# mLSTM gate scans behind the first query and key projection, a gate tile in front of the last head, the last head's end behind the first z tiles

## The chip, the core and the metric

The kernel runs on one core of a Trainium2 chip. The core's engines each work through a queue of their own, in order: TensorE (PE; its weight loads are shown apart, as PEld), VectorE (DVE), ScalarE (ACT), GpSimd (POOL) and SyncE (SP), which only issues transfers. Semaphores tie the queues together. The metric is the time of one execution on the device, in microseconds (us).

## The reference

One layer of a diffusion backbone: 1024 latent tokens and 256 context tokens of width 1024, in float32. The tokens are modulated, projected once into all branch inputs, mixed by a bidirectional mLSTM (8 heads) and a bidirectional gated linear attention (GLA, 4 heads), merged through gates, and passed through a gated convolutional feed-forward network, with two layer norms. The part that matters here is the mLSTM, cut from the reference:

```
q_m, k_m = split(silu(short_conv(concat([q_m, k_m]), conv_qk)))     # 3 taps along the tokens
i_f, i_b, f_f, f_b = transpose(g_m.reshape(b, t, 4, 8))             # 4 gate rows per head
mlstm_gates = ((i_f, log_sigmoid(f_f)), (i_b, log_sigmoid(f_b)))

def step(carry, inp):                        # one chunk of tokens of one head
    b = cumsum(lfc)
    dlog = where(tril, b[:, None] - b[None, :] + lic[None, :], -inf)
    m_inter = b + m
    m_row = maximum(m_inter, dlog.max(-1))
    s = (qc @ kc.T) * exp(dlog - m_row[:, None])
    w_inter = exp(m_inter - m_row)
    num = w_inter[:, None] * (qc @ c_mat) + s @ vc
    den = w_inter * (qc @ n_vec) + s.sum(-1)
    h = num / maximum(abs(den), exp(-m_row))[:, None]
    ...                                      # new c_mat, n_vec, m
y_m = (head_norm(h_m, mlstm_norm_g) * sigmoid(o_m)) @ w_branch_mlstm
y_g = (head_norm(h_g, gla_norm_g) * silu(z_g)) @ w_branch_gla
out = (sigmoid(gate_a) * y_m + sigmoid(gate_b) * y_g) @ w_out
```

## The kernel before

All products of float32 data are made of three: each operand is split into a high part (rounded to the format that TensorE takes) and a low part, and high x high, high x low and low x high are added in one bank of PSUM (`mm3`, lines 279 to 285). The high part of a weight is written by ScalarE (line 252), the low part by VectorE (line 253). `wload` fetches a block of weights as four quarters, through four raw buffers (`raw`) and six buffers each of high and low parts (`whi`, `wlo`). A projection of 128 columns over 512 tokens is 24 products; the context's 256 tokens make 24 of half the width.

PSUM has four kinds of banks with two each: `pj` and `pa` mainly for projections, `pt` for transposes, `po` for the outputs of the heads. A bank is free again when VectorE or ScalarE has read it.

The order of the work is that of the Python code as a list scheduler lays it out: it fills each engine's queue by priority and by when it believes an operand will be ready, so instructions of neighbouring steps are interleaved. On the chip each queue is then fixed, and an instruction that waits holds up all behind it on its engine.

Around the change the code does this:

- Four GLA heads, with gate tiles as filler. A gate tile (`gate_tile`, called by `fill`) projects 128 columns of one of the merge gates over all latent tokens: 48 products, two evacuations on ScalarE (line 537) and two stores. There are 16, four of them here. The last half head of the GLA, `finish`, is kept in the list `rest` and run by `late()`.
- `ml_proj_v(0)`, the values of the first two mLSTM heads (240 products).
- `ml_gates()`: the gate rows of all heads and both directions, on 64 partitions. VectorE makes the running maximum and sum by scans (lines 456 to 462), then `ra` (464), `rr` (466), the key factors `wk` (472, 473; Exp on ScalarE, 474) and the row factors `re` (477, 478). `rr`, `re` and the decays are written to DRAM (489 to 491). TensorE turns three of the row tables by 30 small transposes (501) into `ta`, `twk` and `tem`, which VectorE copies from six `pt` banks (502).
- `ml_proj_qk(h)`, queries and keys of a head: two projections for q, three for k. ScalarE evacuates each (732), VectorE adds two taps of the convolution out of the same bank (727), ScalarE takes the tanh (747) and VectorE multiplies it on (748).
- `ml_scan(h)`: masks and `rr` rows are fetched by GpSimd's queue and added (760, 761), the `re` rows broadcast (764); Exp on ScalarE (765, 769), GpSimd multiplies q (766); TensorE transposes k (777), makes the scores (786), the states (796) and the outputs (816, 817); VectorE normalizes (837). Its last part, `finish`, is given back: eight transposes (844), two scaled copies on ScalarE (845), a store (847).
- The loop over the eight heads projects head h+1, runs the end of head h-1 (`late()`), scans head h, and fills with one or two gate tiles. Then `gated` projects the z tiles (two per block of weights), multiplies the GLA heads with them and splits the products; a stage with the GLA branch weights follows, in which modulation weights are summed on VectorE (906, 908), and later `gated` again for the o gates of the mLSTM heads.

Names in the rows: `s` is any of the numbered slots, `u` the buffers of the tokens, `qq` and `kk` two double slots (row tables first, then the scaled queries and keys of a head), `s<-rmask`, `s<-rr` and `qq<-re` the transfers of a head's masks, rows and row factors.

Of the kernel before, what the change touches and what calls it, by code (L numbers as in the profile page):

```python
# [24 lines left out]
MH = 8  # L25
# [11 lines left out]
def layer_kernel(ctx, tc, I, out, dbg=None):  # L37
# [16 lines left out]
    def nm(s):  # L54
        cnt[0] += 1
        return f"{s}_{cnt[0]}"

    def pt(tag, shape):
        return ps.tile(shape, F32, tag=tag, name=nm(tag))
# [4 lines left out]
    def slot(i, shape, dt=F32):  # L64

        if i in (8, 9, 10, 11) and sl is sl0:
            n = 1
            for w in shape[1:]:
                n *= w
            tag = "kk" if i < 10 else "qq"  # L70
            if i % 2 == 0:
                half[tag] = sl.tile([P, 2, n], dt, tag=tag, name=nm(tag))
            v = half[tag][0:shape[0], i % 2, :]
            return v if len(shape) == 2 else v.rearrange("p (a b) -> p a b", b=shape[2])
        return sl.tile(shape, dt, tag=f"s{i}", name=nm(f"s{i}"))

    def ubt(i, shape, dt=F32):
        return ub.tile(shape, dt, tag=f"u{i}", name=nm(f"u{i}"))
# [35 lines left out]
    for l in range(7):  # L114
        h = 1 << l
# [91 lines left out]
    for i in range(2):  # L207
        hi = stg.tile([P, 2, 256], F32R, tag="whi", name=nm("whi"), bufs=6)
        lo = stg.tile([P, 2, 256], F32R, tag="wlo", name=nm("wlo"), bufs=6)
        h, l = (t[:].rearrange("p a (b c) -> p (a b) c", c=P) for t in (hi, lo))  # L210
# [17 lines left out]
    def cB(i):  # L228
        return colB[:, i:i + 1]
# [21 lines left out]
    def split(hi, lo, src, eng=G):  # L251
        A.activation(hi, src, AF.Copy)  # L252
        eng.tensor_tensor(lo, src, hi.bitcast(F32), op=ALU.subtract)  # L253

    def wload(segs, nk=KD, k0=0, eng=V, into=None):
        parts = []
        for k4 in range(0, nk, 2):
            n = min(2, nk - k4)
            raw = stg.tile([P, 2, 256], F32, tag="raw", name=nm("raw"), bufs=4)
            r0 = (k0 + k4) * P  # L260
            wid = 0
            for src, c0, w, dst in segs:
                SY.dma_start(raw[:, 0:n, dst:dst + w],
                             src[r0:r0 + n * P, c0:c0 + w].rearrange("(k p) c -> p k c", p=P))
                wid = max(wid, dst + w)
            if into is None:
                hi = stg.tile([P, 2, 256], F32R, tag="whi", name=nm("whi"), bufs=6)
                lo = stg.tile([P, 2, 256], F32R, tag="wlo", name=nm("wlo"), bufs=6)
            else:
                hi, lo = (t[k4 // 4][:, k4 % 4:k4 % 4 + 2, :] for t in into)  # L270
            split(hi[:, 0:n, 0:wid], lo[:, 0:n, 0:wid], raw[:, 0:n, 0:wid], eng)
            parts.append((hi, lo))

        def w(k, c, n):
            hi, lo = parts[k // 2]
            return hi[:, k % 2, c:c + n], lo[:, k % 2, c:c + n]
        return w

    def mm3(p, lhs, rhs, nk=KD):
        for k in range(nk):  # L280
            lh, ll = lhs(k)
            rh, rl = rhs(k)
            T.matmul(p, lh, rh, start=k == 0, stop=False)  # L283
            T.matmul(p, lh, rl, start=False, stop=False)  # L284
            T.matmul(p, ll, rh, start=False, stop=k == nk - 1)  # L285
# [29 lines left out]
    def u_tok(t):  # L315
        if t < 8:
            return lambda k: (uh[k][:, t * P:(t + 1) * P], ul[k][:, t * P:(t + 1) * P])
        o = (t - 8) * P
        return lambda k: (cuh[k // 4][:, k % 4, o:o + P], cul[k // 4][:, k % 4, o:o + P])
# [3 lines left out]
    def proj(w, c, b, tag="pj"):  # L323
        p = pt(tag, [P, 512])
        mm3(p[:, 0:BW[b]], lambda k: w(k, c, P), u_blk(b))
        return p
# [183 lines left out]
    def vbias(off):  # L510
        t = sc.tile([P, 256], F32, tag="vb", name=nm("vb"), bufs=2)
        SY.dma_start(t[:], b_in[off:off + 256].unsqueeze(0).to_broadcast([P, 256]))
        return t
# [18 lines left out]
    def gate_tile(dst, off, cb0, j, tags=("pj", "pj")):  # L532
        w = wtile(w_in, off + j * P)
        for b in range(2):
            p = proj(w, 0, b, tags[b])
            t = sc.tile([P, 512], F32, tag="gt", name=nm("gt"), bufs=2)
            A.activation(t[:], p[:], AF.Identity, scale=0.5, bias=cB(cb0 + j))
            A.dma_start(dst[j][:, b * 512:b * 512 + 512], t[:])
# [163 lines left out]
    def ml_proj_v(pr):  # L702
        w = wload([(w_in, O_VM + pr * 256, 256, 0)], eng=V)
        vb = vbias(O_VM + pr * 256)
        vs = [slot(2 + i, [P, 10, 129]) for i in range(2)]
        for t in vs:
            G.memset(t[:, :, 128:129], 1.0)
        for t0 in range(0, 10, 2):
            p = pt("pj", [P, 2, 256])
            for i in range(2):  # L710
                mm3(p[:, i, :], u_tok(t0 + i), lambda k: w(k, 0, 256))
            for e in range(2):
                V.tensor_tensor(vs[e][:, t0:t0 + 2, 0:P], p[:, :, e * P:(e + 1) * P],
                                vb[:, e * P:(e + 1) * P].unsqueeze(1).to_broadcast([P, 2, P]), op=ALU.add)
        return vs
# [136 lines left out]
    def late():  # L852
        while rest:
            rest.pop()()
# [3 lines left out]
    def fill(n, tags=("pj", "pj")):  # L858
        for _ in range(n):
            gate_tile(*gates.pop(0), tags)  # L860
# [10 lines left out]
        if h:  # L871
            fill(1)
    v2 = ml_proj_v(0)
    rr_d, re_d, decb, (ta, twk, tem) = ml_gates()
    qk = ml_proj_qk(0)
    late()
    for h in range(MH):
        nxt = ml_proj_qk(h + 1) if h + 1 < MH else None
        if h and h % 2 == 0:
            v2 = ml_proj_v(h // 2)  # L880
        late()
        rest.append(ml_scan(h, *qk, v2[h % 2]))
        qk = nxt
        fill(2 if h < 2 or h > 5 else 1, ("pj", "pa"))
    late()
    while gates:
        fill(1)

# [6 lines left out]
    def ytag():  # L895
        seq[0] += 1
        return tags[seq[0] % 3]
# [19 lines left out]
    def gated(off, cb0, src_d, silu):  # L917
        hi, lo = [], []
        for j2 in range(4):
            w = wload([(w_in, off + j2 * 256, 256, 0)])  # L920
            for e in range(2):
                j = 2 * j2 + e
                hi.append(slot(j, [P, SEQ], F32R))
                lo.append(slot(8 + j, [P, SEQ], F32R))
                hr = ubt(16 + j % 2, [P, SEQ])
                SY.dma_start(hr[:], src_d[j][:])
                ht = ubt(18, [P, SEQ])
                zz2 = ubt(19, [P, 2, 512]) if silu else None
                for b in range(2):
                    s_ = slice(b * 512, b * 512 + 512)  # L930
                    p = proj(w, e * P, b, ytag())
                    th = sc.tile([P, 512], F32, tag="gt", name=nm("gt"), bufs=2)
                    A.activation(th[:], p[:], AF.Tanh, scale=0.5, bias=cB(cb0 + j))
                    hs = hr[:, s_]
                    if silu:
                        zt = zz2[:, b, :]
                        A.activation(zt, p[:], AF.Identity, scale=0.5, bias=cB(cb0 + j))
                        V.tensor_tensor(hs, zt, hs, op=ALU.mult)
                    V.scalar_tensor_tensor(ht[:, s_], th[:], 1.0, hs, op0=ALU.add, op1=ALU.mult)
                    split(hi[j][:, s_], lo[j][:, s_], ht[:, s_])  # L940
        return hi, lo

    ya_d = [drt(f"ya{j}", [P, SEQ]) for j in range(8)]
    ghi_, glo_ = gated(O_ZG, c_zg, hg_d, True)
    accs = {}
    for j2 in range(4):
# [33 lines left out]
    bup = colF[0][:, 0:44]  # L980
    cb = colF[0][:, 44:66]
    mhi_, mlo_ = gated(O_OM, c_om, hm_d, False)
    xhi, xlo = [], []
    for j2 in range(4):
# [265 lines left out]
    for j, c in enumerate(todo[len(main):]):  # L1250
        if j >= 6:
            if j < 10:
                h = (ubt(10 + j - 6, [P, 2, 512], F32R) if j < 8 else
                     fin.tile([P, 2, 512], F32R, tag="gl", name=nm("wlate"), bufs=2))
                h = [h[:, 0, :], h[:, 1, :]]
            else:
                h = [fin.tile([P, 512], F32R, tag="z1", name=nm("wlate"), bufs=4)[:] for _ in range(2)]
# [40 lines left out]
```

## Time and profile before

| | |
|---|---|
| three runs | 2292.91 us median (2291.26 to 2295.82) |
| the profiled execution | 2294.39 us, of which the span from first to last instruction is 2292.6 |
| TensorE | busy 2235.5 us, 98% of the span; mean granted clock 0.992 |
| VectorE, ScalarE, GpSimd | busy 58%, 32%, 11% |
| transfers | 246.55 MB, 108 GB/s over the span |

A row of the timeline has the start, the time from the first start to the last end, the engine, line and operation, what is written and read, and in brackets how long the engine stood idle before it and whose end released it. TensorE's products overlap: a row of one product shows 0.39 us, but the next one starts 0.23 later. The granted clock is a share of 2.4 GHz; 0.5 is 1.2 GHz.

### The profile page before, as it was taken

How to read it: one execution, taken by the hardware profiler on the slowest of the kernel's cores; microseconds unless marked ns; L12 is line 12 of the kernel's file. 1: busy time of each engine (PE TensorE's matmuls, PEld its weight loads, DVE VectorE, ACT ScalarE, POOL GpSimd, SP SyncE). 2: the span in 40 equal slices, each digit the busy share in tenths (PEclk: the TensorE clock that was granted, in tenths of full speed). 3: DMA queues.
4: the chain of work that ended last, by engine and by line, in shares of the span. 5: the costliest groups of instructions: out<-in, count | busy, mean ns of one | idle time of the engine just before them, and what ended most of it. 6: DMA issues, size and time to landing. Idle time of an engine off the chain costs nothing. (4 is left out here: it accounts for less than half of the span.)

```text
span 2292.6 us, 30337 instructions
## 1 busy us (share of the span) xinstructions
PE 2235.5 (98%) x11641; PEld 1881.5 (82%) x11641; DVE 1321.3 (58%) x2511; ACT 728.8 (32%) x1239; POOL 253.3 (11%) x254
## 2 busy tenths in 40 slices
PE   8989999998999999998999899999999999999998
PEld 4979898987889889897887688787888888888886
DVE  6485737376663665755356523578855656654257
ACT  3563323234233332312431233313333333333110
POOL 1010101021110111101210122102111000000000
PEclk9999999999999999999999999999999999999999
DMA  8231221204332433323358634514311222225731
GB/s 287 69 118 52 60 70 39 67 27 107 88 103 66 119 97 102 101 80 110 96 158 264 206 102 148 192 65 163 113 46 46 65 69 78 74 104 176 216 83 74
DMA packets 187746, 246.55 MB, mean 108 GB/s; under 512 B 16257, under 2 KB 129537, under 8 KB 187601
## 3 DMA queue, kind: packets, MB, share of 16 engines
q1 hardware_dynamic: 164673, 179.16, 25.1%
q0 software_dynamic: 12416, 44.21, 7.3%
q10 hardware_dynamic: 10512, 21.24, 2.5%
q8 instruction: 91, 1.49, 0.3%
q14 instruction: 54, 0.44, 0.1%
HBM read 186.57 MB, written 49.60 MB: 103 GB/s over the span
## 5 line engine op out<-in xcount | busy, mean ns | idle before, releaser
L253 DVE TENSOR_TENSOR wlo<-raw,whi 128x512 fp32r<-128x512 f32 x302 | 216.2, 721 | 166.8 <-ACT whi L252 162.0
L283 PE MATMUL pj<-s,whi 128*128 128x512 f32 x784 | 305.6, 390 | 0.3 <-ACT val L1121 0.3
L285 PE MATMUL pj<-s,wlo 128*128 128x512 f32 x784 | 305.4, 390 | 0.0
L252 ACT ACTIVATE whi<-raw 128x512 fp32r<-128x512 f32 x302 | 188.5, 629 | 337.7 <-PE pj L285 151.8
L284 PE MATMUL pj<-s,whi 128*128 128x512 f32 x744 | 290.4, 390 | 3.0 <-POOL s L1089 2.9
L1145 DVE SCALAR_TENSOR_TENSOR acc<-g,colF,acc 128x945 f32<-128x945 f32 (+2 forms) x168 | 206.4, 1229 | 139.6 <-ACT acc L1136 137.5
L283 PE MATMUL pj<-u,whi 128*128 128x512 f32 (+1 forms) x528 | 207.1, 392 | 4.8 <-ACT whi L252 4.8
L285 PE MATMUL pj<-u,wlo 128*128 128x512 f32 (+1 forms) x528 | 206.2, 391 | 0.0
L284 PE MATMUL pj<-u,whi 128*128 128x512 f32 (+1 forms) x528 | 205.9, 390 | 0.0
L283 PE MATMUL pj<-whi,u 128*128 128x256 f32 x640 | 181.5, 284 | 0.0
L285 PE MATMUL pj<-whi,u 128*128 128x256 f32 x640 | 181.4, 283 | 0.0
L284 PE MATMUL pj<-wlo,u 128*128 128x256 f32 x640 | 181.4, 283 | 0.0
L283 PEld LDWEIGHTS pj<-s,whi 128*128 128x128 f32 x784 | 147.2, 188 | 33.3 <-issue 1.7
L285 PEld LDWEIGHTS pj<-s,wlo 128*128 128x128 f32 x784 | 147.2, 188 | 30.9
L284 PEld LDWEIGHTS pj<-s,whi 128*128 128x128 f32 x744 | 139.7, 188 | 34.3 <-POOL s L1089 4.2
L283 PE MATMUL pa<-u,whi 128*128 128x512 f32 (+1 forms) x376 | 142.1, 378 | 2.2 <-DVE s L727 2.2
L284 PE MATMUL pa<-u,whi 128*128 128x512 f32 (+1 forms) x376 | 141.9, 377 | 0.0
L285 PE MATMUL pa<-u,wlo 128*128 128x512 f32 (+1 forms) x376 | 141.2, 376 | 0.0
L284 PEld LDWEIGHTS pj<-wlo,u 128*128 128x128 f32 x640 | 122.8, 192 | 0.0
L283 PEld LDWEIGHTS pj<-whi,u 128*128 128x128 f32 x640 | 122.8, 192 | 0.1
L285 PEld LDWEIGHTS pj<-whi,u 128*128 128x128 f32 x640 | 122.8, 192 | 0.0
L283 PEld LDWEIGHTS pj<-u,whi 128*128 128x128 f32 x528 | 100.2, 190 | 24.1 <-ACT whi L252 5.2
(500 smaller groups left out, 4361.9 us busy)
## 6 DMA issues: line engine op xcount, KB each, us to landing
u<-in_w_mod_dram SPq DMA_DIRECT2D x48, 512.0 KB
raw<-in_w_in_dram SPq DMA_DIRECT2D x96, 256.0 KB
raw<-in_w_up_dram SPq DMA_DIRECT2D x176, 128.0 KB
raw<-in_w_in_dram SPq DMA_DIRECT2D x96, 128.0 KB
raw<-in_w_down_dram SPq DMA_DIRECT2D x44, 256.0 KB
s<-rmask POOLq DMA_DIRECT2D x16, 512.0 KB, 4.7
s<-rr POOLq DMA_DIRECT2D x16, 512.0 KB, 8.7
qq<-re POOLq DMA_DIRECT2D x16, 512.0 KB, 6.6
```

The costliest lines, as they stand in the source:

```text
L252: A.activation(hi, src, AF.Copy)
L253: eng.tensor_tensor(lo, src, hi.bitcast(F32), op=ALU.subtract)
L283: T.matmul(p, lh, rh, start=k == 0, stop=False)
L284: T.matmul(p, lh, rl, start=False, stop=False)
L285: T.matmul(p, ll, rh, start=False, stop=k == nk - 1)
L1145: V.scalar_tensor_tensor(av, g[:, r0 + dy:r1 + dy, c0 + dx:c1 + dx], convw(3 * ky + kx, f), av, op0=ALU.mult, op1=ALU.add)
```

## The change

```diff
@@ -871,18 +871,19 @@
         if h:
             fill(1)
     v2 = ml_proj_v(0)
-    rr_d, re_d, decb, (ta, twk, tem) = ml_gates()
     qk = ml_proj_qk(0)
     late()
+    rr_d, re_d, decb, (ta, twk, tem) = ml_gates()
     for h in range(MH):
         nxt = ml_proj_qk(h + 1) if h + 1 < MH else None
         if h and h % 2 == 0:
             v2 = ml_proj_v(h // 2)
+        if h == MH - 1:
+            fill(1, ("pj", "pa"))
         late()
         rest.append(ml_scan(h, *qk, v2[h % 2]))
         qk = nxt
-        fill(2 if h < 2 or h > 5 else 1, ("pj", "pa"))
-    late()
+        fill(2 if h < 2 or h == 6 else 1, ("pj", "pa"))
     while gates:
         fill(1)
@@ -938,6 +939,7 @@
                         V.tensor_tensor(hs, zt, hs, op=ALU.mult)
                     V.scalar_tensor_tensor(ht[:, s_], th[:], 1.0, hs, op0=ALU.add, op1=ALU.mult)
                     split(hi[j][:, s_], lo[j][:, s_], ht[:, s_])
+            late()
         return hi, lo
```

Three edits. `ml_gates()` is called after the first head's queries and keys and the end of the last GLA head. The last head's two gate tiles are parted: one ahead of the end of head 6, one after the scan of head 7. The end of head 7 is run by `gated` after its first block, two z tiles. The count of gate tiles and products is the same. Between the two places, and behind the second, the queues are as they were.

On TensorE the gate transposes (line 501) of before stand among the first products of head 0 (banks `pj_4736` and `pa_4767`); this piece has the last four of the six, `s_699` being `wk` and `kk` the Exp of the running maximum:

```order
L283 MATMUL pa_4767<-u_46_299,whi_4710 128x512
L284 MATMUL pa_4767<-u_54_307,whi_4710 128x512
L285 MATMUL pa_4767<-u_46_299,wlo_4711 128x512
L283 MATMUL pa_4767<-u_47_300,whi_4710 128x512
L501 MATMUL pt_4678<-ident,s_699_4638 128x64 x8
L501 MATMUL pt_4688<-ident,s_699_4638 128x64 x2
L284 MATMUL pa_4767<-u_55_308,whi_4710 128x512
L285 MATMUL pj_4736<-u_50_303,wlo_4725 128x512
L283 MATMUL pj_4736<-u_51_304,whi_4724 128x512
L284 MATMUL pj_4736<-u_59_312,whi_4724 128x512
L501 MATMUL pt_4693<-ident,kk_4613 128x64 x8
L501 MATMUL pt_4703<-ident,kk_4613 128x64 x2
```

After the change head 0's projections stand together, and the transposes come among the first products of head 1 (`pj_4949`), behind the end of the GLA (line 692):

```order
L692 MATMUL pt_4804<-ident,hn_4817 128x128
L284 MATMUL pj_4949<-u_54_307,whi_4923 128x512
L285 MATMUL pj_4949<-u_46_299,wlo_4924 128x512
L283 MATMUL pj_4949<-u_47_300,whi_4923 128x512
L501 MATMUL pt_4876<-ident,s_728_4828 128x64 x8
L284 MATMUL pj_4949<-u_55_308,whi_4923 128x512
L501 MATMUL pt_4886<-ident,s_728_4828 128x64 x2
L285 MATMUL pj_4949<-u_47_300,wlo_4924 128x512
L283 MATMUL pj_4949<-u_48_301,whi_4930 128x512
L284 MATMUL pj_4949<-u_56_309,whi_4930 128x512
L501 MATMUL pt_4891<-ident,s_729_4851 128x64 x8
L501 MATMUL pt_4901<-ident,s_729_4851 128x64 x2
```

On VectorE the end of the gate operations, with the splits of weights (line 253) around it, is this before (`wlo_4725` and `wlo_4732` are the third and fourth quarter of head 0's weights):

```order
L472 TENSOR_TENSOR s_699_4638<-s_698_4615,qq_4614 32x1280
L473 TENSOR_TENSOR s_699_4638<-s_698_4615,qq_4614 32x1280
L713 TENSOR_TENSOR s_689_4354<-pj_4562,vb_4352 128x2x128
L713 TENSOR_TENSOR s_690_4355<-pj_4562,vb_4352 128x2x128
L477 TENSOR_TENSOR kk_4613<-qq_4614,kk_4613 32x1152
L478 TENSOR_TENSOR kk_4613<-qq_4614,kk_4613 32x1152
L502 COPY ta<-pt_4663 128x128
L502 COPY ta<-pt_4673 128x32
L253 TENSOR_TENSOR wlo_4725<-raw_4721,whi_4724 128x512
L253 TENSOR_TENSOR wlo_4732<-raw_4728,whi_4731 128x512
```

And after:

```order
L472 TENSOR_TENSOR s_729_4851<-s_728_4828,qq_4827 32x1280
L253 TENSOR_TENSOR wlo_4631<-raw_4627,whi_4630 128x512
L713 TENSOR_TENSOR s_689_4354<-pj_4562,vb_4352 128x2x128
L713 TENSOR_TENSOR s_690_4355<-pj_4562,vb_4352 128x2x128
L253 TENSOR_TENSOR wlo_4638<-raw_4634,whi_4637 128x512
L473 TENSOR_TENSOR s_729_4851<-s_728_4828,qq_4827 32x1280
L477 TENSOR_TENSOR kk_4826<-qq_4827,kk_4826 32x1152
L478 TENSOR_TENSOR kk_4826<-qq_4827,kk_4826 32x1152
L253 TENSOR_TENSOR wlo_4924<-raw_4920,whi_4923 128x512
L253 TENSOR_TENSOR wlo_4931<-raw_4927,whi_4930 128x512
```

The scans ahead of these rows are in the same places in both. The two splits of head 0 have gone ahead of lines 473 to 478, and the table copies (502) come far later, behind head 0's taps.

On ScalarE the first head of before begins with Exps of masked rows (769) between the evacuations of head 0's projections (732):

```order
L481 ACTIVATE dec<-kk_4613 32x9
L482 ACTIVATE dec<-kk_4613 32x9
L483 ACTIVATE kk_4613<-kk_4613 64x1280
L769 ACTIVATE s_763_5127<-s_763_5127,ta 128x128 x2
L732 ACTIVATE s_718_4735<-pj_4736,cvb,colB 128x512
L769 ACTIVATE s_763_5127<-s_763_5127,ta 128x128 x6
L765 ACTIVATE qq_5110<-qq_5110 128x1024 x2
L732 ACTIVATE s_718_4735<-pa_4767,cvb,colB 128x512
L769 ACTIVATE s_761_5112<-s_761_5112,ta 128x128 x7
L747 ACT_TABLE_LOAD
L747 ACTIVATE s_722_4798<-s_718_4735 128x1024
L769 ACTIVATE s_761_5112<-s_761_5112,ta 128x128
```

And after:

```order
L481 ACTIVATE dec<-kk_4826 32x9
L732 ACTIVATE s_708_4641<-pj_4642,cvb,colB 128x512
L482 ACTIVATE dec<-kk_4826 32x9
L483 ACTIVATE kk_4826<-kk_4826 64x1280
L732 ACTIVATE s_708_4641<-pa_4673,cvb,colB 128x512
L765 ACTIVATE qq_5110<-qq_5110 128x1024 x2
L747 ACT_TABLE_LOAD
L747 ACTIVATE s_712_4704<-s_708_4641 128x1024
L732 ACTIVATE s_713_4707<-pa_4708,cvb,colB 128x512
L732 ACTIVATE s_713_4707<-pj_4739,cvb,colB 128x512
```

The Exps of the row factors (765) now stand between q's evacuations and its tanh, with k's evacuations behind; the Exps of line 769 follow after the first evacuation of head 1. GpSimd's queue has been turned about in the same way: the two broadcasts (764) and the two products (766) first, the masks and rows (760, 761) behind them.

On ScalarE the end of head 6 (845) stood behind two splits for the z weights and one evacuation of a gate tile:

```order
L769 ACTIVATE s_1313_9433<-s_1313_9433,ta 128x128 x6
L252 ACTIVATE whi_9796<-raw_9794 128x512
L252 ACTIVATE whi_9802<-raw_9800 128x512
L537 ACTIVATE gt_9399<-pa_9374,colB 128x512
L845 ACTIVATE s_1306_9402<-pt_9403,colB 128x512
```

And after:

```order
L769 ACTIVATE s_1323_9501<-s_1323_9501,ta 128x128 x6
L252 ACTIVATE whi_9782<-raw_9780 128x512
L252 ACTIVATE whi_9788<-raw_9786 128x512
L537 ACTIVATE gt_9399<-pa_9374,colB 128x512
L538 DMA tha_863<-gt_9399 128x512
L537 ACTIVATE gt_9439<-pj_9414,colB 128x512
L538 DMA tha_864<-gt_9439 128x512
L252 ACTIVATE whi_9794<-raw_9792 128x512
L252 ACTIVATE whi_9800<-raw_9798 128x512
L537 ACTIVATE gt_9467<-pa_9442,colB 128x512
L845 ACTIVATE s_1316_9470<-pt_9471,colB 128x512
```

The parted gate tile's two evacuations and the third and fourth quarter of the first z weights (`whi_9794`, `whi_9800`) have come in between. On TensorE that gate tile's 48 products stand ahead of the transposes of line 844, with the rows behind those in the same order as before.

## Rows read from the trace of the kernel before

**Rows 1.** The core's span and clock, and the page's list of engines.
```profile
core 0: 2292.6 us, clock 0.992
...
PE 2235.5 (98%) x11641; PEld 1881.5 (82%) x11641; DVE 1321.3 (58%) x2511; ACT 728.8 (32%) x1239; POOL 253.3 (11%) x254
```

**Rows 2.** Waits of TensorE, by releaser: us in total, times, longest.
```profile
PE pa L618 <- DVE qq L626: 8.2, 13, 1.5
PE pt L777 <- ACT s L845: 5.8, 1, 5.8
...
PE pt L501 <- DVE ta L502: 3.2, 1, 3.2
...
PE pa L283 <- DVE s L727: 2.2, 1, 2.2
```

**Rows 3.** Timeline of TensorE at the start of head 0's projections.
```profile
527.19 0.81 PE L501 MATMUL pt<-ident,s 64*128 64x64 f32 x10 [0.55 <-ACT whi L252]
...
528.73 0.40 PE L283 MATMUL pj<-u,whi 128*128 128x512 f32 x1
528.96 0.39 PE L284 MATMUL pj<-u,whi 128*128 128x512 f32 x1
```

**Rows 4.** Windows: length, busy time per engine, clock, DMA share, GB/s.
```profile
156.00:500.00 344.00, 333.06 (x2125) 296.18 (x2124) 203.39 (x375) 107.08 (x218) 41.27 (x46) 1.00 0.17 50
536.00:558.00 22.00, 19.84 (x75) 15.29 (x74) 6.63 (x18) 11.29 (x23) 3.80 (x5) 0.77 0.68 175
1049.00:1056.00 7.00, 4.70 (x23) 4.70 (x24) 4.22 (x8) 2.82 (x6) 0.73 (x1) 0.52 0.57 187
```

**Rows 5.** Timeline of VectorE from 530 to 558 us.
```profile
530.14 1.48 DVE L473 TENSOR_TENSOR s<-s,qq 32x1280 f32<-32x1280 f32 x1
...
533.69 1.35 DVE L478 TENSOR_TENSOR kk<-qq,kk 32x1152 f32<-32x1152 f32 x1
...
535.49 1.29 DVE L253 TENSOR_TENSOR wlo<-raw,whi 128x512 fp32r<-128x512 f32 x2
...
546.18 1.54 DVE L727 SCALAR_TENSOR_TENSOR s<-pj,colB,s 128x511 f32<-128x511 f32 x2 [6.37 <-ACT s L732]
...
557.58 1.23 DVE L748 SCALAR_TENSOR_TENSOR s<-s,s 128x1024 f32<-128x1024 f32 x1 [4.34 <-ACT s L747]
```

**Rows 6.** Transfers, issue to landing: of `gm_d`, `re`, `rr`, `rmask`, in this order.
```profile
DMA to landing us min/median/max: 1.7/2.3/2.6
...
DMA to landing us min/median/max: 3.6/6.6/10.1
...
DMA to landing us min/median/max: 6.1/8.7/9.9
...
DMA to landing us min/median/max: 3.9/4.7/8.4
```

**Rows 7.** Timeline of ScalarE from 549 to 557 us.
```profile
549.62 1.06 ACT L765 ACTIVATE qq<-qq 128x1024 f32<-128x1024 f32 x1 [0.48 <-DMA qq<-re]
550.59 0.76 ACT L732 ACTIVATE s<-pa,cvb,colB 128x512 f32<-128x512 f32 x1
...
555.19 1.28 ACT L747 ACT_TABLE_LOAD   x1
```

**Rows 8.** Timeline of ScalarE before the end of head 6.
```profile
1048.97 1.13 ACT L252 ACTIVATE whi<-raw 128x512 fp32r<-128x512 f32 x2
...
1050.58 0.67 ACT L845 ACTIVATE s<-pt,colB 128x512 f32<-128x512 f32 x1
```

**Rows 9.** Timeline of TensorE at the end of head 6.
```profile
1043.54 1.03 PE L844 MATMUL pt<-ident,s 128*128 128x128 f32 x8
...
1051.30 0.69 PE L777 MATMUL pt<-ident,s 128*128 128x128 f32 x2 [5.83 <-ACT s L845]
```

**Rows 10.** Timeline of SyncE near 1182 us, and of TensorE near 1284 us.
```profile
1182.19 0.39 SPq L906 DMA_DIRECT2D u<-in_w_mod_dram  x1
...
1284.46 0.80 PE L283 MATMUL pj<-u,whi 128*128 128x512 f32 x1 [4.80 <-ACT whi L252]
```

## The prediction

> **What bounds the kernel now.** I read the list of engines first: TensorE is busy 98% of the span [rows 1], so only its idle stretches and its slow ones can be won. Then the waits of TensorE [rows 2]: sorted by releaser, the list shows thirteen short ones in the linear-attention scans (line 618, none over 1.5 us) and a few long single ones. Two belong to this change's first place, around 527 to 558 us: 3.2 us of the gate transposes (line 501) for a copy on VectorE, and 2.2 us of the first key projection for its bank, which the tap products (line 727) must have read. One belongs to its second place: 5.8 us of the last head's key transposes (line 777) for ScalarE's copy of the head before (line 845). The timeline adds 0.55 us ahead of the first gate transpose [rows 3]. Last the busy times by window, for the clock [rows 4]: from 156 to 500 us it is 1.00 in spite of the thirteen short waits; between 536 and 558 it averages 0.77, and from 1049 to 1056 0.52, so after the 3.2, 2.2 and 5.8 us waits TensorE ran a while at 1.2 instead of 2.4 GHz.
>
> **What can be won.** First place: waits 0.55 + 3.20 + 2.17 = 5.9 us, and clock (1 - 0.77) x 22 = 5.1 us. Second place: the wait 5.8 us; of the 7 us window TensorE works 4.70, nearly all at 1.2 GHz, so half of that, 2.3 us, is lost. Together 19.1 us.
>
> **First edit: the gates behind the first query and key projection.** No instruction is added or removed. The order shows that on VectorE the scans stay where they were (so it is only in part what the words of the change say); what moves is the gate transposes on TensorE, from ahead of and between the first products of head 0 to between the first products of head 1, over 100 products later, and what ScalarE and GpSimd do for head 0. All three old waits lose their cause: the transposes come long after the scans' end, and the Exps that wait for the mask and row transfers (line 769) no longer stand ahead of the evacuations of head 0. Four things are late next.
>
> (a) The low parts of the weights' third and fourth quarter now stand between the gate operations on VectorE. TensorE goes straight on at 527.19 - 0.55 = 526.64. With a step of 0.23 us [rows 3] it wants the third quarter's low part for its 15th product, at 526.64 + 14 x 0.23 = 529.9. VectorE is then in line 472, which ends where line 473 starts now, 530.14; the split takes half of 1.29 [rows 5]: 530.8. Wait 1.0 us; none if that line came two places earlier, 1.5 if one more operation got in between.
>
> (b) On ScalarE the two Exps of the row factors (line 765) now stand ahead of the tanh of q and of the evacuation of the first key projection, and they wait for a broadcast. Line 478 ends at 533.69 + 1.35 = 535.0 now, and 1.29 later, 536.3, behind the two splits [rows 5]. The row is written to DRAM and read again: 2.3 us for a transfer of that size (`gm_d`) and 6.6 for the broadcast, both medians [rows 6]: 545.2. Then Exp 1.06, the table load 1.28, the tanh, as large as that Exp, 1.06 [rows 7]: 548.6; on VectorE line 748 with 1.23 and two taps with 1.54 [rows 5]: 551.4. Only then is the bank free that the context's key projection wants. TensorE comes to it after 96 products from 526.64 and the 1.0 us of (a), at 549.7. Wait 1.7 us. With the fastest broadcast (3.6) everything is 3 us earlier, and the projection's own end decides, some 547.0, with its evacuation of 0.76 [rows 7] and the taps: 549.3, no wait. With the slowest (10.1) the wait is 5.2, and 2.3 are lost to the clock as after the 5.8 us one: 7.5. I take 1.7: two broadcasts with some weights beside them are nearer to the median than to the crowd of masks, rows and weights that runs at this place now, with the transfer engines 0.68 busy [rows 4]. For the clock I take nothing: 1.7 lies between waits of 1.5 us, which left it alone, and 2.2, which did not.
>
> The Trainium skill (DMA: Bandwidth & Descriptors, section on the anatomy of a software-descriptor DMA) gives such a transfer about 2.0 us plus its bytes at 436 GB/s, by my estimate 3.2 us for 512 KB. The rows disagree: one landed in 3.6, the median is 6.6. By the page the wait of (b) would be nothing and the whole gain 1.7 us larger.
>
> (c) The gate tables now go through two small banks between single products, each copied by VectorE with weight splits queued among the copies (half of 1.29 each). Four hand-overs, from 0 to 4 x 0.65 = 2.6 us; I take 0.8, because one to three products stand between them.
>
> (d) The mask and row transfers of head 0 are now issued behind GpSimd's two products, and wait for the gate transposes, whose sources they overwrite; the last Exps wait for them with an evacuation of head 1 queued behind. The transposes are done about 560; then mask 4.7 and row 8.7 [rows 6]: 573.5, Exps, evacuation and taps to 578. TensorE wants that bank after three more projections, about 580: nothing, with 2 us to spare. With the slowest of both rows (8.4 and 9.9) it waits some 3 us.
>
> **Second edit: a gate tile ahead of the last head.** 48 products of 0.23 = 11 us come before the transposes of head 6, and one gate tile fewer comes after the scan; the sum of products is the same. ScalarE is free of its Exps at about 1049 now [rows 8], so the end of head 6 will find it free when the transposes come at 1043.54 + 11 = 1054.5 [rows 9]. But in front of line 845 the order now has the fourth quarter of the z weights, whose buffer is freed only by the gate tile's last products, and that tile's own evacuation: 0.6 + 0.67 + 0.67 = 1.9 us after the tile's end [rows 8], against 1.03 for the eight transposes and about 0.5 for four of the score products. Wait 0.4 to 0.6; I take 0.6, from 0.3 to 1.5, all too short for the clock by what the windows show.
>
> **Third edit: the last head's end behind two z tiles.** Eight transposes and two copies change place. Nothing waits for the head's store before the o gates, a whole stage on; the z tiles rotate through three kinds of banks with two each, so 1.3 us more on ScalarE is hidden by over 5 us of products per tile half. If that cover were gone, it would cost those 1.3 us.
>
> **Sum.** 19.1 - (1.0 + 1.7 + 0.8 + 0.6) = 15.0 us. The profiled execution took 2294.39 us with a span of 2292.6; the median of the three runs is 2292.91, 1.5 lower. Taken off the median: 2277.9 us.
>
> **Rivals.**
> *The broadcast holds ScalarE* (b at its upper end). For it: a broadcast has taken 10.1 us [rows 6], and an Exp of this head waited for one [rows 7]. Against: masks and rows shared the queue then, and are now issued later. The gain falls by 7.5 - 1.7 = 5.8: 2283.7.
> *A later stage takes it back: no change.* There is a 4.8 us wait near 1284 [rows 10], behind a stage whose modulation weights come through two buffers, a DMA at a time. If that chain began at a fixed time, TensorE would only arrive earlier and wait longer: 2292.9. Against: its loads start at 1182, in buffers that the z tiles hold to their end, so it moves with them.
> *Slower: the clock stays low.* Place: from the wait of (b) at 549.7, through the gate transposes between single products, to the end of head 1's projections. Work that takes 1 us at 2.4 GHz costs 1 us more at 1.2; the five projections of head 1, 96 products and 24 of half the width, are 108 x 0.23 = 24.8 us. If they all ran so, 2277.9 + 24.8 = 2302.7; it is slower than before from 15 us of such work on. Against: thirteen short waits left the clock at 1.00 [rows 4]. The Trainium skill (TensorE: Matmul & The Clock Gate, section on psum-queue depth-cycling) tells of a kernel whose frequent micro-idles between groups of products made the clock swing; the trace of the scans here disagrees, but their waits were never as dense as those of (c) can be.
>
> **How the numbers follow.** My forecast 0.78, with a range of its own from 2273 (new waits of 0.3 us in all, 2274.1, and the runs' scatter) to 2283; the broadcast 0.12; no change 0.06; slower 0.04. What can be told from no change is 0.2%, 4.6 us: faster means under 2288.3, slower over 2297.5. The broadcast's case is still faster; with the last Exps of (d) on top it comes to 2287 and, in the worst case, into the band, which takes 0.02 from faster. Faster 0.88, same 0.08, slower 0.04. The range, 2273 to 2288, leaves out the last two rivals.
>
> **What would show it.** The three old waits gone from TensorE's list; a wait of about 1 us for line 253 near 530; a wait for line 727 or 737 near 550, with its length read beside the landing of the row factors' broadcast, from 0 to 5 us; short waits for line 502 near 558; under 1.5 us for line 845 near 1040; and the clock at 1.00 from 500 to 1250. Wrong would be a new wait over 3 us, a low clock in either place, or a 1284 wait that has grown by what was gained.

## The result, and the profile after

| | before | after |
|---|---|---|
| first comparison, 6 runs each | 2293.04 us (2291.26 to 2295.82) | 2280.32 us (2277.97 to 2282.36) |
| ratio of the two | | 0.9942, 95% interval 0.9932 to 0.9953 |
| the profiled execution | 2294.39 us | 2277.97 us |
| its span, mean granted clock | 2292.6 us, 0.992 | 2276.2 us, 0.997 |

The change is 12.7 us faster, with an interval from 10.8 to 15.6; 2277.9 was predicted. The profiled execution of after is the fastest of its six, so the two traces differ by more, 16.4 us.

First the core and the list of engines, as in [rows 1]: TensorE has 6.4 us less of busy time for the same 11641 products.

```profile
core 0: 2276.2 us, clock 0.997
...
PE 2229.1 (98%) x11641; PEld 1876.1 (82%) x11641; DVE 1322.5 (58%) x2511; ACT 728.4 (32%) x1239; POOL 253.3 (11%) x254
```

Then the waits of TensorE, as in [rows 2] (releaser, then us in total, times, longest). The waits for lines 502, 727 and 845 are gone. In their place stand three of about 1 us: the low part of head 0's third quarter (`wlo`), the context's key projection, which waits for the copy of an edge column (`ed`, line 737) out of its bank, and the last transposes of the GLA (692), which wait for VectorE's line 690. The wait before the o gates, 4.8 us in [rows 10], is 4.0.

```profile
PE pa L618 <- DVE qq L626: 8.4, 13, 1.7
...
PE pj L283 <- ACT whi L252: 4.0, 1, 4.0
...
PE pt L692 <- DVE hn L690: 1.2, 1, 1.2
...
PE pa L283 <- DVE ed L737: 1.1, 1, 1.1
PE pj L285 <- DVE wlo L253: 0.9, 1, 0.9
```

And windows (length, busy time of each engine, clock, DMA share, GB/s), to be held against [rows 4]: at the first place the clock was 0.77 and is 1.00, and from there to 1250 us nothing lowers it.

```profile
526.00:558.00 32.00, 28.82 (x145) 23.02 (x144) 24.63 (x40) 15.44 (x21) 5.83 (x4) 1.00 0.32 87
558.00:1250.00 692.00, 691.73 (x3971) 597.95 (x3972) 398.03 (x1084) 218.70 (x432) 95.32 (x89) 1.00 0.42 121
```

To see where time went, without what differs between any two executions, I take the distance between the starts of two products that stand in every trace: the last of line 618 and the first score of head 0 (786) around the first place; the first score of head 6 and the first row sum of the modulation around the second.

| us | before | after | after, traced again | first edit alone | second alone | third alone |
|---|---|---|---|---|---|---|
| first place | 109.4 | 102.8 | 103.5 | 102.6 | 109.0 | 109.1 |
| second place | 192.5 | 184.4 | 184.4 | 192.4 | 185.0 | 192.8 |
| from there to the end of TensorE | 1083.3 | 1081.8 | 1083.2 | 1083.3 | 1080.3 | 1085.1 |

The places gain 6.6 and 8.1 us, together 14.7 (14.0 in the second trace of the same kernel). The last row, in which the queues are alike, varies by up to 4.8 us between traces; the difference between 14 and the medians' 12.7 is no more than that.

### The profile page after: what moved, and what is told of

Same layout as the page of the kernel before. It is cut to its first block, busy times and chain, and to the rows that moved or that the text cites. A ratio compares the mean times of both kernels' runs of the same rounds, so it can differ in the third digit from the quotient of the medians.

```text
span 2276.2 us, 30329 instructions
## 1 busy us (share of the span) xinstructions
PE 2229.1 (98%) x11641; PEld 1876.1 (82%) x11641; DVE 1322.5 (58%) x2511; ACT 728.4 (32%) x1239; POOL 253.3 (11%) x254
## 4 chain that ended last, share of the span: by engine, by line
PE 86%; DVE 6%; DMA 5%; ACT 1%; issue 1%; POOL 0%; SPq 0%; DVEq 0%; ACTq 0%; POOLq 0%
PE pj L285 16%; PE pj L283 16%; PE pj L284 16%; PE pa L283 4%; PE pa L284 4%; PE pa L285 4%; DMA u<-in_w_mod_dram 2%; PE pa L618 2%; PE pt L796 1%; PE po L816 1%; PE po L817 1%; PE po L284 1%; PE po L285 1%; PE po L283 1%; PE pt L659 1%
```

## The experiments

All times are medians; "before" ran on the same chip beside them (2293.41 us for the first four, 2293.49 for the next four, 2293.95 for the last two).

**The three edits apart, and all of them again.**

```diff
 # e1: the gates only
-    rr_d, re_d, decb, (ta, twk, tem) = ml_gates()
     qk = ml_proj_qk(0)
     late()
+    rr_d, re_d, decb, (ta, twk, tem) = ml_gates()
 # e2: the gate tile only
+        if h == MH - 1:
+            fill(1, ("pj", "pa"))
         late()
 ...
-        fill(2 if h < 2 or h > 5 else 1, ("pj", "pa"))
+        fill(2 if h < 2 or h == 6 else 1, ("pj", "pa"))
 # e3: the end of head 7 only, from behind the loop into gated
-    late()
     while gates:
 ...
+            late()
         return hi, lo
```

> The first edit alone (the gate scans' call behind head 0's projections and the end of the GLA). Theory (every place pays by itself, waits and clock both): the waits of 5.9 us and the 5.1 us of clock at 527 to 558 go, and three new waits come, 0.9 us for a low part, 1.1 for the context's key projection and 1.2 for the GLA's last transposes (read from the trace of the changed kernel): gain 7.8 us, about 2285.2. The 5.8 us wait near 1051 stays, followed by a stretch at 0.5. Rival A (the clock gives nothing back, only the waits count): gain 2.7 us, about 2290.3. Rival B (a later stage takes back what an early place gains): no gain, 2293.

> The second edit alone (one of the last head's two gate tiles ahead of it; the end of head 7 stays after the loop). Theory: the 5.8 us wait and the 2.3 us of clock near 1051 go, with no new wait at the place: gain 8.1 us, about 2284.9; the waits of 0.55, 3.2 and 2.2 us at 527 to 558 stay, with the clock at 0.77 there. Rival A (waits alone count): gain 5.8, about 2287.2. Rival B (the wait before the o gates, 4.8 us in the trace of before, grows by what is gained): 2293, and that wait at 10 us or more.

> The third edit alone (the end of head 7 run behind the first two z tiles). Theory: worth nothing, 2293 within 0.2%, and no wait of TensorE over 0.5 us between 1100 and 1200. Rival: its two copies on ScalarE and eight transposes delay a z tile, 1.3 us slower, 2294.3; or the end of head 7 did hold TensorE up and it is up to 1.3 us faster. With all three alone, the sum of the gains by the theory is 15.9; by a rival in which the places share one later wait it is more than the gain of the three together.

> The changed kernel once more, beside the three edits alone, on the same chip. Theory: its gain is the sum of the three, 15.9 us as read from its traced execution (2277 us); the runs so far give 12.7 (10.8 to 15.6). If the sum is right, the missing 3 us are in waits and clock stretches that differ between executions: the 4.7 us wait near 145 with a low clock after it for 3.4 us in one trace and 6.8 in the other, and the 4 us wait near 1266. If the places are not independent, the gain stays near 12.7 while e1 and e2 give 7.8 and 8.1.

| | us | ratio to before, 95% interval |
|---|---|---|
| e1, gates only | 2288.61 (11 runs) | 0.9977, 0.9968 to 0.9986 |
| e2, gate tile only | 2285.53 (5) | 0.9963, 0.9951 to 0.9976 |
| e3, end of head 7 only | 2293.02 (11) | 0.9995, 0.9986 to 1.0004 |
| e4, all | 2279.86 (5) | 0.9938, 0.9924 to 0.9951 |

The edits add up: 4.8 + 7.9 + 0.4 = 13.1 us against 13.6 for all (medians). So the places are independent as far as the scatter lets one see, and what the second gained is not paid back before the o gates: in the trace of e2 that wait is 3.8 us, not 10. The clock's part is real too: at its place e2 gains 7.5 us in the trace, with a wait of 5.8 (the medians alone, 5.5 to 11.2, would not tell). e1's gain of 4.8 us (interval 3.2 to 7.3) is under the 7.8 expected. Its place gained 6.8 in the trace, and the reason for the missing 1 us is in the next section; the interval takes in 6.8, and for the 2 us between trace and median no cause is shown. e3 is nothing, as expected. e4's list of TensorE's waits has the one for line 737 at 1.7 us instead of 1.1:

```profile
PE pa L283 <- DVE ed L737: 1.7, 1, 1.7
```

and its window over the place (columns as above) still shows a clock of 1.00:

```profile
526.00:600.00 74.00, 69.57 (x379) 57.71 (x379) 49.26 (x99) 30.51 (x51) 9.48 (x8) 1.00 0.39 101
```

**The broadcast taken away from ScalarE's queue.**

```diff
 # e5, in ml_gates: Exp once on the table; in ml_scan: none on the broadcast rows
-        A.activation(dec[0:32, 1:10], re3[0:32, 1:10, P - 1], AF.Exp)
+        A.activation(re3[0:32, 1:10], re3[0:32, 1:10], AF.Exp)
+        V.tensor_copy(dec[0:32, 1:10], re3[0:32, 1:10, P - 1])
 ...
-            A.activation(ee, ee, AF.Exp)
```

> The changed kernel, but the Exp of the row factors is taken once, on the table before it is written to DRAM, and not on the broadcast rows of each head; so ScalarE no longer waits for the broadcast between q's evacuations and q's tanh. Theory (ScalarE's wait for the broadcast, standing ahead of the tanh and of k's evacuations, makes the wait for the context's key projection): that wait near 550, 1.1 and 1.7 us in two traces of the changed kernel, falls to 0 to 0.3, since the bank's own end at 546.8 with an evacuation of 0.76, two taps of 1.53 and a copy of 0.15 gives 549.2 against TensorE's 549.5. The GLA's last transposes behind it wait 0 to 0.8 instead of 1.2, since VectorE's queue is earlier. Gain on the changed kernel 1.1 to 2.5 us, about 2278. Rival: the bank waits for its own products and VectorE's line, not for ScalarE: the wait stays above 0.8.

2277.46 us (5 runs, 2275.52 to 2279.09), ratio 0.9928 (0.9916 to 0.9940): the fastest kernel of the study, 2.4 us under e4, in another comparison. The intervals of the two overlap, so the gain rests on the traces: the first place takes 100.6 us instead of 102.8 and 103.5. On ScalarE the evacuation of the first key projection now follows its products, and TensorE's list has neither of the two waits:

```profile
542.66 1.06 ACT L747 ACTIVATE s<-s 128x1024 f32<-128x1024 f32 x1
547.00 0.78 ACT L732 ACTIVATE s<-pa,cvb,colB 128x512 f32<-128x512 f32 x1 [3.28 <-PE pa L285]
```

The theory holds, at the upper end of its gain.

**The two products of head 0 on VectorE.**

```diff
-            G.tensor_tensor(ee, ee, q[:], op=ALU.mult)
+            (G if h else V).tensor_tensor(ee, ee, q[:], op=ALU.mult)
```

> The changed kernel with the two products of head 0 (line 766) on VectorE instead of GpSimd; they stand ahead of the taps of the first key projection. Theory of two parts: (1) what stands ahead of the taps on VectorE is paid in full: the wait near 550 grows by the two products, 2 x 1.2, to 3.5 to 4 us; (2) the split of weights at 552 us that took 2.19 us instead of 0.68, and the one-column subtraction that took 0.99 instead of 0.15, were slowed by GpSimd's product beside them, both with two operands from SBUF: they take 0.7 and 0.2 now, and the GLA's last transposes wait under 0.5 us instead of 1.2. Rival to (2): the split is slow for another reason (its operands come late, transfers beside it): still over 1.5 us. In all 1 to 4 us slower than the changed kernel, with the clock low after the longer wait.

One run, 2282.84 us, with 105.5 us at the first place. Both parts hold. The wait for line 690 is gone, and TensorE's list shows the grown one:

```profile
PE pa L283 <- DVE s L743: 3.6, 1, 3.6
```

VectorE's timeline has the split at its usual length,

```profile
555.79 0.69 DVE L253 TENSOR_TENSOR wlo<-raw,whi 128x512 fp32r<-128x512 f32 x1 [1.46 <-ACT whi L252]
```

and the window behind the wait has a lowered clock, 0.66:

```profile
553.00:558.00 5.00, 4.31 (x24) 4.34 (x25) 3.01 (x9) 1.88 (x3) 0.00 (x0) 0.66 0.07 9
```

**Modulation loads on GpSimd's queue, and then only the first block of the o gates' weights.**

```diff
 # e7, in mod_sum
-            SY.dma_start(raw[:], I["w_mod"][...])
+            G.dma_start(raw[:], I["w_mod"][...])
 # e9 (on top of e5), in gated; dq is the queue that wload issues on
-            w = wload([(w_in, off + j2 * 256, 256, 0)])
+            w = wload([(w_in, off + j2 * 256, 256, 0)], dq=None if silu or j2 else G)
```

> The changed kernel with the modulation weights' loads (32 of 512 KB, in the stage ahead of the o gates) issued by GpSimd's queue instead of SyncE's. Theory (SyncE's queue stands behind a load that waits for its buffer, and the o gates' weights are late for that): the 4.0 us wait near 1266 and the half clock after it (3.4 or 6.8 us of it, 1.7 to 3.4 lost) go: gain 5 to 7 us, about 2274. Rival A: the modulation chain itself is the pace (two buffers, VectorE's sums), so TensorE waits as long for the row sums' transposes: no gain, 2280. Rival B: GpSimd's queue serves such loads more slowly than SyncE's: slower, 2283 or more.

> As e5 (the Exp of the row factors taken once), and the first block of weights for the o gates (four loads of 256 KB) is issued by GpSimd's queue; the modulation weights stay on SyncE's. Theory (the wait before the o gates is the order of SyncE's queue: their weights stand behind modulation loads that wait for a buffer): the wait of 4.0 to 4.5 us near 1265 and its stretch at half clock (3.4 or 6.8 us, half of it lost) go, and the modulation chain keeps its pace of 12.3 us a row: gain 5.7 to 7.9 us on e5's 2277.5, about 2270.5. Rival A: the modulation chain is the pace, and the wait moves to the row sums' transposes: 2277 or more. Rival B: the zeroing of the sums, on GpSimd behind these loads, starts the chain later: waits of 1 to 3 us for the row sums from 1230 on, 2280.

e7: 2295.83 us (11 runs), 1.0010 (1.0001 to 1.0019), 15 to 16 us slower than the changed kernel. e9: 2281.10 (5 runs), 0.9945 (0.9932 to 0.9959), 3.6 slower than e5; the intervals of these two overlap, but in the traces the stretch from the first row sum to the end of TensorE is 5.9 us longer in e9. Both took the wait for the weights (`whi`) away, and both got waits for the row sums (914) instead. First e7's list:

```profile
PE pt L914 <- DVE u L909: 15.4, 5, 6.1
```

its modulation loads from issue to landing,

```profile
DMA to landing us min/median/max: 4.2/5.0/7.7
```

and e9's list:

```profile
PE pt L914 <- DVE u L909: 7.7, 4, 3.6
```

My theory of this wait falls: with the weights there in time, TensorE waits for the row sums, so the chain of modulation loads through two buffers sets the pace (rival A of both; the time of e7 is that of its rival B), and weights that go ahead of it (e9) only move the wait. In e7 the sums of a row end 14 to 16 us apart on VectorE, in the changed kernel 12 to 14. A load takes 5.1 us from issue to its first sum there against 4.8, and GpSimd issues it 0.30 us behind the release of its buffer, SyncE 0.03: with two loads per buffer and row, some 1.2 of the 2.1 us that a row is longer; for the rest no cause is shown. e9 came near the time of its rival B (2280), but not by its cause: in its trace each zeroing on GpSimd (902) waited for a transfer, not for the loads ahead of it. That the two buffers and not the transfer engines limit the chain is argued, not shown: those are 0.80 busy from 1230 to 1280 us in the changed kernel, and more buffers were not tried.

**The second edit's means at another place.**

```diff
 # e8, h == 0 of the GLA loop; the mLSTM loop
-            fill(1)
+            fill(2)
-        fill(2 if h < 2 or h == 6 else 1, ("pj", "pa"))
+        fill(2 if h < 1 or h == 6 else 1, ("pj", "pa"))
```

> The second edit's means at another place: the changed kernel with a second gate tile ahead of the first GLA scan, taken from the two after head 1. Theory (a gate tile of 11 us ahead of a wait of 4.7 us takes the wait and the low clock after it, at a place where ScalarE and VectorE are done by then): the 4.7 us wait near 145 and its 3.4 to 6.8 us at half clock (1.7 to 3.4 lost) go: gain 6.4 to 8 us, about 2273. Rival A: head 1 needs its second tile, and a wait of 3 us or more comes there, near 650 to 750: gain under 4. Rival B: VectorE's queue is the pace of the first scan, and the wait only moves behind the tile: 2280.

2287.64 us (9 runs), 0.9974 (0.9964 to 0.9984): 7 to 8 us slower than the changed kernel. Rival B was nearest. The wait at 145 is gone, and head 1 does not miss its tile; but the first scan's levels now follow one another with waits of 1.7, 2.6, 3.2 and 1.9 us. The list of waits for that line:

```profile
PE pa L618 <- DVE qq L626: 13.4, 12, 3.2
```

and the window over the first levels, where the clock falls:

```profile
150.00:180.00 30.00, 20.54 (x113) 18.24 (x112) 26.82 (x43) 8.27 (x15) 10.48 (x9) 0.83 0.10 26
```

VectorE is busy 26.8 of these 30 us, and 28.7 in the changed kernel: the scan goes at its pace. What differs is the filler: in the changed kernel 7 to 11 projection products stand on TensorE ahead of each of the four levels (618) behind the first, in e8 none. So the tile fills one wait, and the products behind it meet the others without filler. Ahead of head 7 it worked because ScalarE was done by then.

**Key factors on GpSimd.**

```diff
 # e10 (on top of e5), both directions
-        V.tensor_tensor(wk3[0:32], ra3[0:32], ...)
+        G.tensor_tensor(wk3[0:32], ra3[0:32], ...)
```

> As e5, and the two sums of the key factors (lines 472 and 473, 32 x 1280) run on GpSimd instead of VectorE, so the splits of head 0's third and fourth quarter come 1.5 us sooner in VectorE's queue. Theory (term (a): the 0.92 us wait near 530 is VectorE's queue alone): the wait goes, with the 0.27 us that TensorE's restart costs; about 2276.3 against 2277.5. Rival (VectorE and GpSimd hold each other up when both read two operands from SBUF): the additions and splits of VectorE beside GpSimd's sums take 1.3 to 2.2 us instead of 0.7 and 1.35, the wait stays at 0.5 to 2 us, and the time is the same or some 1 us longer.

2280.54 us (5 runs), 0.9940 (0.9928 to 0.9953): 3.1 slower than e5, more than the rival said; the two intervals overlap a little, and at the first place the traces differ by 2.3 us (102.9 against 100.6). First GpSimd's sums in its timeline:

```profile
527.86 4.05 POOL L472 TENSOR_TENSOR s<-s,qq 32x1280 f32<-32x1280 f32 x1 [22.94 <-DVE qq L466]
531.99 2.68 POOL L473 TENSOR_TENSOR s<-s,qq 32x1280 f32<-32x1280 f32 x1
```

Then VectorE beside them: two splits take 3.42 us instead of 1.29, line 478 takes 2.72 instead of 1.35 [rows 5], and TensorE waits twice for a low part (0.8 and 1.1 us) and 1.2 us for a bank that the taps (727) must have read.

```profile
529.04 3.42 DVE L253 TENSOR_TENSOR wlo<-raw,whi 128x512 fp32r<-128x512 f32 x2
...
533.16 2.72 DVE L478 TENSOR_TENSOR kk<-qq,kk 32x1152 f32<-32x1152 f32 x1
```

## Why the prediction was right, point by point

**The removable 19.1 us.** Nearly all of it went, 18.6: the three long waits and both low clocks are gone, as the windows show. Between the products at the first place the start-to-start distances beyond those at full clock had 4.6 us of low clock, against the 5.1 of the term.

**(a), the third quarter's low part.** Predicted 1.0 near 530; 0.92 at 530.38, for line 253, and 0.9 in every trace with the edit but e10's. The queue was read rightly to 0.1 us.

**(b), ScalarE behind the broadcast.** Predicted 1.7 from 549.7; the traces of the changed kernel have 1.1 and 1.7, that of e1 0.9. ScalarE's timeline of after has the events in the order of the forecast: two Exps that wait for a transfer, the table load, the tanh, the evacuation.

```profile
541.72 1.06 ACT L765 ACTIVATE qq<-qq 128x1024 f32<-128x1024 f32 x1 [2.50 <-DMA qq<-re]
544.23 1.06 ACT L765 ACTIVATE qq<-qq 128x1024 f32<-128x1024 f32 x1 [1.45 <-DMA qq<-re]
545.31 1.28 ACT L747 ACT_TABLE_LOAD   x1
546.61 1.06 ACT L747 ACTIVATE s<-s 128x1024 f32<-128x1024 f32 x1
547.57 0.76 ACT L732 ACTIVATE s<-pa,cvb,colB 128x512 f32<-128x512 f32 x1
```

The second row landed at 544.2, 6.0 us after its issue at 538.2; I had 6.6 from 538.6. In e4 it took 6.6, from 538.16 to 544.78, and there the wait was the 1.7 of the forecast, so the wait follows the landing; ScalarE's timeline of e4:

```profile
544.78 1.06 ACT L765 ACTIVATE qq<-qq 128x1024 f32<-128x1024 f32 x1 [1.10 <-DMA qq<-re]
```

The Trainium skill's price for such a transfer (DMA: Bandwidth & Descriptors, section on the anatomy of a software-descriptor DMA) gave 3.2 us by my estimate; 6.0 and 6.6 agree with the rows of before and not with that. e5 shows that the wait hangs on this queue. For the clock I took nothing, and the clock stayed at 1.00 after 1.1 and 1.7 us; after a wait of 3.6 (e6) it did not. That was in part luck, for the length of one wait does not settle it. In e8 a wait of 1.65 us in the first scan was followed by a clock of 0.5, and so was one of 1.46 in the last:

```profile
468.71 0.42 PE L618 MATMUL pa<-qq,s 128*128 128x128 f32 x1 [1.46 <-ACT s L612]
```

The window behind it (columns as above) has a mean clock of 0.57:

```profile
470.00:474.00 4.00, 4.00 (x16) 3.58 (x15) 2.92 (x6) 1.48 (x3) 2.20 (x2) 0.57 0.00 0
```

In e4 a longer one, ahead of a row sum, left it at 1.00:

```profile
1262.46 0.59 PE L914 MATMUL pt<-u,ones 128*1 128x512 f32 x1 [1.89 <-DVE u L909]
```

and its window:

```profile
1262.50:1267.00 4.50, 3.92 (x14) 2.23 (x14) 2.46 (x4) 0.25 (x1) 0.00 (x0) 1.00 0.77 229
```

**(c), the gate transposes between products.** This term failed in its mechanism: 0.8 us of waits for banks were predicted, and the list of TensorE's products shows none. Yet the place lost about as much in another way, so that the size was right by luck. TensorE's timeline of after shows time lost at each change between products and transposes:

```profile
556.25 0.39 PE L285 MATMUL pj<-u,wlo 128*128 128x512 f32 x1
556.48 0.40 PE L283 MATMUL pj<-u,whi 128*128 128x512 f32 x1
556.85 0.71 PE L501 MATMUL pt<-ident,s 64*128 64x64 f32 x8
557.48 0.50 PE L284 MATMUL pj<-u,whi 128*128 128x512 f32 x1
557.91 0.33 PE L501 MATMUL pt<-ident,s 64*128 64x64 f32 x2
558.18 0.50 PE L285 MATMUL pj<-u,wlo 128*128 128x512 f32 x1
558.51 0.40 PE L283 MATMUL pj<-u,whi 128*128 128x512 f32 x1
```

A product's next start is 0.23 later as a rule; here it is 0.37 and 0.43 later ahead of a transpose (556.48 to 556.85, 557.48 to 557.91) and 0.33 after one (558.18 to 558.51). The weight loads of TensorE, which have rows of their own, name a bank for the first of these groups:

```profile
556.84 0.57 PEld L501 LDWEIGHTS pt<-ident,s 64*128 64x128 f32 x8 [0.41 <-ACT s L695]
```

ScalarE had read that bank at 556.79, so of the excess of 0.14 us there a part may be a wait. The banks of the other three groups had been read 0.3 to 0.6 us before, so their excess of 0.1 to 0.2 us is no wait for a bank; why a change costs it is not shown. Summed from 526 us to the end of the first place, such excess is 2.5 us in after and 1.7 in before, which has as many waits but three groups of these transposes instead of four: 0.8 us more. That closes the account: waits 5.9 and clock 4.6 gone, 3.2 of new waits and 0.8 of breaks come: 6.5, and the distance between the products gives 6.6.

**(d), masks and rows behind the products.** Nothing was predicted, and nothing came: ScalarE's last Exps of head 0 end about 577, and TensorE does not wait. In the second trace of the kernel (e4) it waits just behind this place, at 586.5, for VectorE's scaled keys, which no step had; in after that wait is absent, and its cause is open:

```profile
PE pt L777 <- DVE kk L780: 0.7, 1, 0.7
```

**A wait that no step had.** The GLA's last transposes wait 1.2 us for line 690, at 555.7. VectorE is late there, because two of its operations met GpSimd's products. First GpSimd's row of after (two products in one row, each about half of it):

```profile
549.01 4.75 POOL L766 TENSOR_TENSOR qq<-qq,s 128x1024 f32<-128x1024 f32 x2 [10.28 <-DVE s L748]
```

Then VectorE's timeline beside it:

```profile
548.84 1.53 DVE L727 SCALAR_TENSOR_TENSOR s<-pa,colB,s 128x511 f32<-128x511 f32 x2
...
550.40 0.99 DVE L743 TENSOR_TENSOR s<-s,cvb 128x1 f32<-128x1 f32 x1
551.32 0.74 DVE L727 SCALAR_TENSOR_TENSOR s<-pj,colB,s 128x511 f32<-128x511 f32 x1
552.11 2.19 DVE L253 TENSOR_TENSOR wlo<-raw,whi 128x512 fp32r<-128x512 f32 x1
...
555.21 0.47 DVE L690 TENSOR_SCALAR hn<-pa,gss 128x256 f32<-128x256 f32 x1
```

The one-column subtraction (line 743, 0.15 alone) ends at 551.39, with the first product; the split (0.68 alone) ends at 554.30, half a microsecond after the second product's end at 553.76. Together 2.3 us are lost. With the products on VectorE (e6) or earlier (e5) line 690 is in time and the wait is gone: shown.

**The second edit.** Predicted 8.1 less 0.6; 8.1 came, and no new wait. The copies of line 845 did start late, behind the split and the evacuation of the tile, as forecast; ScalarE's timeline of after:

```profile
1048.04 0.67 ACT L537 ACTIVATE gt<-pa,colB 128x512 f32<-128x512 f32 x1
1048.61 0.68 ACT L845 ACTIVATE s<-pt,colB 128x512 f32<-128x512 f32 x1
```

But TensorE had eight score products (1.06 us) between the transposes, where I counted four; TensorE's timeline:

```profile
1047.53 1.04 PE L844 MATMUL pt<-ident,s 128*128 128x128 f32 x8
1048.40 1.06 PE L786 MATMUL pa<-s,s 128*128 128x128 f32 x8
1049.34 0.44 PE L777 MATMUL pt<-ident,s 128*128 128x128 f32 x2
```

**The third edit** is nothing, by e3.

**The sum and the rivals.** Forecast 15.0, at the places 14.0 to 14.7, in the medians 12.7 and 13.6. That the new costs came to 4.0 us where 4.1 were added up is in part luck: the 1.2 us that no step had stand against 0.6 too many in (b) and the 0.6 that the second edit did not cost, and the 0.8 of (c) came by another way. The broadcast's two rows took 4.7 and 6.0 us (5.6 and 6.6 in e4), far from the 10.1 of that rival. "A later stage takes it back" is refuted by e2 and by the wait before the o gates, which moved along and did not grow. The clock did not stay low at this place; e8 shows the thing itself, four waits of 1.7 to 3.2 us close together and a clock of 0.83.

## What to carry to other kernels

Read the loss of a wait with the slow clock behind it, and then the new order of every queue, instruction by instruction: the waits of (a) and (b) came out to 0.1 and 0.6 us by adding durations along one engine's queue. A filler tile helps ahead of a wait whose releaser will be done by the tile's end (head 7), not ahead of a stage that runs at another engine's pace and then lacks the filler between its own steps (e8). And an instruction that waits for a transfer should not stand in a queue ahead of evacuations: moving an Exp to the small table, ahead of the broadcast, was worth 2.4 us more in the medians and 2.2 to 2.8 at its place.

## What was not expected of the hardware

VectorE and GpSimd stop each other. In the trace of after, of VectorE's splits of weights, which read two operands from SBUF, the 283 that start beside no GpSimd arithmetic take 0.68 us, none over 0.70; the 19 that start beside it take 0.72 to 2.19. The taps of line 727, with one operand in PSUM, take 0.75 beside it and 0.75 elsewhere. The Trainium skill (SBUF — State Buffer, section on who interferes with whom) says that a VectorE instruction with two SBUF inputs and a GpSimd instruction that reads SBUF exclude each other, and that the later one blocks until the first ends. The traces agree: each blocked operation above ends no later than its usual length after GpSimd's, and in e10 GpSimd's first sum, issued during VectorE's line 477, took 4.05 us, the second 2.68. One split of e10 that starts within the row of that first sum, at 529.04, takes its usual 0.67, so GpSimd did not hold VectorE up through all of such a row.
